# A diffusion trunk's GLA layers: level products at plain priority, larger first shares, gates dealt out between states

## The chip, the cores and the metric

The kernel runs on one core of a Trainium2 chip, as one launch. The metric is device time in microseconds, the median of several runs.

## The reference, cut to what matters

The model is a trunk of four layers over 512 latent and 256 context tokens of width 1024. Layer i uses mixer i % 3: layers 0 and 3 are gated linear attention (GLA), layer 1 is windowed attention, layer 2 a gated linear recurrence. Only the GLA layers are touched here. Each has four heads with keys of 128 and values of 256, and runs in both directions:

```python
la_f, la_b = [split_heads(jax.nn.log_sigmoid(((h @ w_g1[d]) @ w_g2[d] + b_g[d])) / GLA_TAU, GLA_HEADS) for d in range(2)]
...
def step(s, inp):
    q_n, k_n, v_n, b_n = inp
    rel = b_n[:, :, :, None, :] - b_n[:, :, None, :, :]
    decay = jnp.exp(jnp.where(lower, rel, -jnp.inf))
    scores = jnp.einsum('bhtd,bhsd,bhtsd->bhts', q_n, k_n, decay)
    o = scores @ v_n + (q_n * jnp.exp(b_n)) @ s
    b_last = b_n[:, :, -1:, :]
    s = jnp.exp(b_last)[:, :, 0, :, None] * s + jnp.swapaxes(k_n * jnp.exp(b_last - b_n), -1, -2) @ v_n
    return s, o
...
return (o.astype(z.dtype) * jax.nn.silu(z)) @ w_out
```

In layer 0 latent and context tokens both give an output; in layer 3 the context only gives the state that the latent tokens start from.

## The kernel before

All large products are made of three matmuls on a high and a low part of each operand, so each weight tile is split after its load: ScalarE copies the high half (line 266), VectorE or, for every third tile, GpSimd subtracts to get the low half (line 269). While `keep_pool` holds something, GpSimd gets none of these splits. Weight tiles `raw` and `wh`/`wl` have two buffers each.

A GLA layer (`gla`, from line 937 on) goes through its heads one after the other, and overlaps the outputs of one head with the preparation of the next:

- `gates(h)` (line 958): two small products per head and direction into two banks of PSUM (line 976), |x| and min(x, 0) (lines 980, 981), Exp, Ln, a subtraction (lines 982 to 984), a ladder of pairwise sums for the levels (line 987), and two more Exp (lines 988, 990). It gives the decay factors `tmp` and `ls`.
- `project(h)` (line 995): q and k, in three parts; the parts are q and k of the context (in layer 3 k alone), q of the latent tokens, and k of the latent tokens. `Y` holds k twice, once for each direction.
- `levels` (line 1038): the scores within a chunk of 128 are built from eight levels, of 1, 2, ... 128 tokens. `X` is q times a factor (line 1043). At each level up to 128, ScalarE copies k into `K` (line 1090, levels 2 to 16), TensorE makes many small products of 32 columns (`products`, line 1056, into the banks `sct`), and VectorE multiplies X and Y by the level's factors (line 1105). Then A is put together with masks on VectorE, GpSimd and ScalarE (lines 1116 to 1136).
- `outputs` (line 1138) of the head before: five pairs of transposes of Y (`turn`, line 1150) with copies to `kth` and `ktl` (lines 1152, 1153); five state products (`step`, line 1160) with their updates; then chunk products of A, values, X and states (line 1188), normalisation, and transposes into the output.
- `values(h)` and `zgates(h - 1)` (the silu gate z, line 395) are large products that are dealt out between the levels by `spread`: it hands each level a share of them and traces that share in front of the level's own instructions.
- `mods`: parts of the modulation products for later layers, whose weights come by DMA and whose matmuls have raised priority.

The order of work is not written out by hand here. Instructions are traced in the order of the Python code; a scheduler at build time fills each engine's queue, and takes of those instructions that it holds to be ready the one that was traced first. `tc.high_priority(n)` moves instructions up by n places in that order. On the chip each queue is then worked off strictly in that order, and an instruction that waits holds up all behind it on its engine. In the main loop before, `gates(h)` is called ahead of the projection and the states of the last head; `among` then runs two parts of the projection ahead of the outputs and one after the first state, and the level products are traced with priority 300.

Of the kernel before, what the change touches and what calls it, by code (L numbers as in the profile page):

```python
# [11 lines left out]
F32 = mybir.dt.float32  # L12
# [3 lines left out]
ALU = mybir.AluOpType  # L16
# [19 lines left out]
BURST = 300  # L36
# [41 lines left out]
def body(ctx: ExitStack, tc: tile.TileContext, I, out, layers=(0, 1, 2, 3)):  # L78
    nc = tc.nc
    V, S, G, PE = nc.vector, nc.scalar, nc.gpsimd, nc.tensor  # L80
# [59 lines left out]
    ps = pjt()  # L140
# [73 lines left out]
    keep_pool = []  # L214
# [77 lines left out]
    def load_g2(a, zero=True, load=True):  # L292

        r = gpt.rearrange("p j n -> p (j n)")[:, 0:1024].rearrange("p (d n) -> p d n", d=2)
        if a in g2_loaded:
            return r
        if zero:
            (V if a == 0 else G).memset(r, 0.0)
        if load:
            g2_loaded.append(a)  # L300
            for d in range(2):
                for g in range(3):
                    (nc.sync if d else nc.scalar).dma_start(
                        r[32 * g + 16 * d : 32 * g + 16 * d + 16, d, :], I["a_w_g2"][a, d]
                    )
        return r
# [281 lines left out]
    def run(steps):  # L588
        for _ in steps:
            pass  # L590
# [346 lines left out]
    def gla(i, a, ctx_out):  # L937
# [2 lines left out]
        TOT = 2 * T  # L940
        with phase(f"gla{i}") as mp:

            g2r = load_g2(a)
            w1 = weights("g1")
            t1 = mp.tile([P, T], F32R, name="t1")
            for stream in ("ctx", "lat"):
                t0, n = STREAM[stream]
# [6 lines left out]
            g2 = mp.tile([P, 2, 512], F32R, name="g2")  # L954
            S.copy(g2[:96], g2r[:96])
            G.tensor_tensor(g2[32:64], g2r[32:64], g2[32:64].bitcast(F32), op=ALU.subtract)

            def gates(h):


                tmp = mp.tile([P, 2, T], F32, name="tmp", tag="tmp")
                ls = mp.tile([P, TOT], F32, name="ls", tag="ls")

                def lev(n):
                    if n == 0:
                        return tmp
                    return ls[:, OFF[n] : OFF[n] + 2 * NLEV[n]].rearrange("p (d n) -> p d n", d=2)

                l1 = ls.rearrange("p (d n) -> p d n", d=2)
                for pl in range(2):  # L970
                    d = 1 - pl
                    b = sm[:, 48 + 8 * a + 4 * d + h : 49 + 8 * a + 4 * d + h]
                    ps = sct().rearrange("p c n -> p (c n)")
                    for stream in ("ctx", "lat"):
                        t0, n = STREAM[stream]
                        PE.matmul(
                            ps[:, t0 : t0 + n], g2[:96, d, h * P : (h + 1) * P], t1[:96, t0 : t0 + n],
                            start=True, stop=True,
                        )
                    S.activation(tmp[:, pl, :], ps[:, :T], AF.Abs, bias=b)  # L980
                    V.tensor_scalar(l1[:, pl, :], ps[:, :T], b, 0.0, op0=ALU.add, op1=ALU.min)
                S.activation(tmp, tmp, AF.Exp, scale=-1.0)
                S.activation(tmp, tmp, AF.Ln, bias=1.0)
                V.tensor_tensor(tmp, l1, tmp, op=ALU.subtract)
                for n in range(len(LEVELS) - 1):
                    s = lev(n).rearrange("p d (m two) -> p d m two", two=2)
                    V.tensor_tensor(lev(n + 1), s[:, :, :, 0], s[:, :, :, 1], op=ALU.add)
                S.activation(tmp, tmp, AF.Exp, scale=1.0 / 16.0)
                n = OFF[-1] + 2 * NLEV[-1]
                S.activation(ls[:, :n], ls[:, :n], AF.Exp, scale=1.0 / 16.0)  # L990
                tl = mp.tile([P, 2, NLEV[-1]], F32, name="tl", tag="tl", bufs=2)
                V.tensor_copy(tl, lev(len(LEVELS) - 1))
                return (tmp, ls), tl

            def project(h, q, Y):
                w = weights(f"qk{h}")
# [41 lines left out]
            def levels(ls, q, Y, X, A):  # L1038
# [42 lines left out]
                for n, L in enumerate(LEVELS):  # L1081
                    dims = ([2 * L, 16 // L], [T + L, 2], [1, L])
                    Ks = []
                    for chunks in groups if L < 128 else ():
                        k0, kn = chunks[0] * P, len(chunks) * P
                        if L == 1:
                            K = Y[:, 0, k0 : k0 + kn]
                        elif L <= 16:
                            K = mp.tile([P, 3 * P], F32, name="K", tag="K", bufs=2)
                            S.copy(K[:, :kn], view(Yf, k0, ([2 * L, kn // (2 * L)], [T + L, 2], [1, L])))  # L1090
                        else:
                            K = None
                        Ks.append((chunks, K))
                    with tc.high_priority(BURST):
                        for gi, (chunks, K) in reversed(list(enumerate(Ks))):
                            products(L, dims, tl[gi], chunks, K)
                    if L < 128:
                        N = NLEV[n]
                        lf = ls[:, OFF[n] : OFF[n] + 2 * N] if n else l1.rearrange("p d n -> p (d n)")

                        def up(Z, nt, off, step):
                            m = nt // (2 * L)
                            z = view(Z, 0, ([2 * L, m], [T + L, 2], [1, L]))
                            t = view(lf, off, ([2, m], [step, 2], [0, L]))
                            V.tensor_tensor(z, z, t, op=ALU.mult)

                        up(Xf, nq, 1, N - 1)
                        up(Yf, T, N + 1, -N - 1)
                    yield
# [28 lines left out]
            def outputs(h, X, Y, A, v, tl):  # L1138
# [5 lines left out]
                kt = {}  # L1144

                def turn(m):
                    ps = mxt()
                    for pl in range(2):
                        c = order[pl][m]
                        PE.transpose(ps[:, pl * P : (pl + 1) * P], Y[:, pl, c * P : (c + 1) * P], ident)  # L1150
                    kt[m] = [mp.tile([P, 256], F32R, name=n, tag=n, bufs=2) for n in ("kth", "ktl")]
                    S.copy(kt[m][0], ps[:, :256])
                    V.tensor_tensor(kt[m][1], ps[:, :256], kt[m][0].bitcast(F32), op=ALU.subtract)

                def step(m):
                    k = kt.pop(m)
# [85 lines left out]
            def mods(n):  # L1242
                for _ in range(n):
                    background(1)
                    yield
# [4 lines left out]
                    for stream in ("ctx", "lat") if ctx_out else ("lat",):  # L1250
                        yield from z_steps(mp, w, e, 2 * h + e, put, (stream,))

            def among(main, side, every, lead=0):

                for _ in range(lead):
                    next(side, None)
                for n, _ in enumerate(main):
                    if n in every:
                        next(side, None)

            def spread(main, side, steps, total):

                credit = 0
                for _ in range(steps):
                    credit += total / steps
                    while credit > 0:
                        credit -= next(side, 1e9)
                    next(main)
                run(main)

            put = {}
            prev = None
            keep_pool.append(1)
            for h in range(GH):
                ls, tl = gates(h)
                q = mp.tile([P, T], F32, name="q", tag="q")
                Y = mp.tile([P, 2, T], F32, name="Y", tag="Y", bufs=2)
                pr = project(h, q, Y)
                os = outputs(*prev) if prev else iter(())
                z = zgates(h - 1) if prev else iter(())  # L1280
                among(os, pr, [0, 3, 6], 2)
                run(pr)
                run(mods(3))
                X = mp.tile([P, 2, T], F32, name="X", tag="X")
                A = [mp.tile([P, 6, P], F32R, name=n, tag=n) for n in ("Ah", "Al")]
                lv = levels(ls, q, Y, X, A)

                if h < GH - 1:
                    OG.b = None
                    vl = OG.tail(F32R)  # L1290
                else:
                    vl = mp.tile([P, 2, T], F32R, name="vl", tag="tmp")
                v = (
                    mp.tile([P, 6, GDV], F32R, name="v", tag="v"),
                    vl.rearrange("p d t -> p (d t)").rearrange("p (c n) -> p c n", c=6),
                )

                side = chain(z, values(h, v))
                nz = len(STREAM) * T if ctx_out else len(STREAM) * TL
                nz = nz if prev else 0  # L1300
                spread(lv, side, len(LEVELS), 24 * (nz + 4 * GDV) / 2.4)
                run(side)
                run(mods(2))
                prev = (h, X, Y, A, v, tl)
# [459 lines left out]
```

## Time and profile before

| | |
|---|---|
| median of 3 runs | 1525.08 us (1524.38 to 1532.94) |
| the profiled execution | 1530.24 us |
| its span | 1528.5 us |
| TensorE busy | 1449.4 us (95%) |
| VectorE busy | 1013.6 us (66%) |
| ScalarE busy | 786.9 us (51%) |
| GpSimd busy | 190.5 us (12%) |
| mean granted TensorE clock | 0.983 |

The page gives for each engine its busy time and share of the span; a wait is named by the engine that sat idle and by the instruction that released it. All positions are microseconds from the span's start. In rows, PE is TensorE, DVE is VectorE, ACT is ScalarE, POOL is GpSimd and SP the queue that issues most DMAs; `L1160` is line 1160. PEclk is the granted clock, 1.00 for 2.4 GHz and 0.50 for 1.2 GHz. Layer 0's GLA runs from about 62 to 375 us, layer 3's from about 1225 to 1478 us.

### The profile page before, as it was taken

The numbers are of one execution on the slowest core, as the hardware profiler recorded it, in microseconds if no ns is written. First come the engines' busy times: TensorE is split into PE (matmuls) and PEld (weight loads), VectorE is DVE, ScalarE is ACT, GpSimd is POOL, SyncE is SP. The second block draws the span as 40 slices with busy tenths as digits, with TensorE's granted clock in tenths as the row PEclk, the third lists the DMA queues.
The fourth block names the chain that finished last, engine by engine and source line by source line (L and its number), as shares of the span: only waits on it lengthen the run. The fifth ranks groups of instructions, "written<-read, shape, count | busy, mean of one in ns | idle before, by whom it ended". The sixth has DMA issues, their size and how long they took to land.

```text
span 1528.5 us, 29077 instructions
## 1 busy us (share of the span) xinstructions
PE 1449.4 (95%) x11691; PEld 1213.7 (79%) x11691; DVE 1013.6 (66%) x1913; ACT 786.9 (51%) x1543; POOL 190.5 (12%) x301
## 2 busy tenths in 40 slices
PE   5998899999999899999999999899999889999998
PEld 3877788888877777878888787788878778879886
DVE  5585647576264389787883568988962666766754
ACT  4644353524252357655662477878842555355242
POOL 2211101012122200010000210000011311101111
PEclk8999999999999999999999999999999999999999
DMA  9450514112573632122216624212251352121132
GB/s 304 138 149 18 170 56 143 56 33 70 206 235 128 183 94 70 43 66 56 56 45 226 216 82 150 82 49 70 66 188 50 102 158 88 33 59 56 60 110 84
DMA packets 153046, 162.35 MB, mean 106 GB/s; under 512 B 12418, under 2 KB 141968, under 8 KB 152912
## 3 DMA queue, kind: packets, MB, share of 16 engines
q1 hardware_dynamic: 147456, 146.56, 31.0%
q10 hardware_dynamic: 5456, 13.94, 2.5%
q8 instruction: 92, 1.51, 0.4%
q14 instruction: 42, 0.34, 0.1%
HBM read 138.44 MB, written 11.53 MB: 98 GB/s over the span
## 4 chain that ended last, share of the span: by engine, by line
PE 51%; DVE 10%; ACT 7%; DMA 5%; issue 2%; SPq 1%; POOL 1%; ACTq 0%; DVEq 0%; POOLq 0%
PE mxt L796 15%; PE pjt L395 9%; PE pjt L385 6%; PE pjt L1028 4%; PE mxt L1525 3%; PE mxt L1509 2%; DMA raw<-in_w_mod_dram 2%; PE mxt L524 2%; PE sct L1630 2%; PE mxt L1468 1%; PE mxt L1188 1%; PE mxt L1451 1%; DVE wl L269 1%; ACT wh L266 1%; PE mxt L638 1%
## 5 line engine op out<-in xcount | busy, mean ns | idle before, releaser
L385 PE MATMUL pjt<-Rh,wh 128*128 128x256 f32 (+1 forms) x592 | 198.6, 337 | 7.1 <-DVE Rh L649 4.6
L385 PE MATMUL pjt<-Rl,wh 128*128 128x256 f32 (+1 forms) x592 | 198.1, 336 | 2.1 <-DVE Rl L650 1.8
L385 PE MATMUL pjt<-Rh,wl 128*128 128x256 f32 (+1 forms) x592 | 197.2, 334 | 0.7 <-DVE wl L269 0.7
L269 DVE TENSOR_TENSOR wl<-raw,wh 128x1024 fp32r<-128x1024 f32 x105 | 128.4, 1231 | 56.8 <-ACT wh L266 56.4
L266 ACT CAST wh<-raw 128x1024 fp32r<-128x1024 f32 x118 | 122.0, 1053 | 80.8 <-PE mxt L796 33.0
L395 PE MATMUL pjt<-Rl,wh 128*128 128x512 f32 (+1 forms) x448 | 162.0, 362 | 0.0
L395 PE MATMUL pjt<-Rh,wh 128*128 128x512 f32 (+1 forms) x448 | 161.6, 361 | 0.0
L395 PE MATMUL pjt<-Rh,wl 128*128 128x512 f32 (+1 forms) x448 | 161.3, 360 | 0.0
L796 PE MATMUL mxt<-wh,Rh 128*128 128x512 f32 x352 | 138.9, 395 | 0.0
L796 PE MATMUL mxt<-wh,Rl 128*128 128x512 f32 x352 | 137.6, 391 | 0.8 <-DVE Rl L769 0.8
L796 PE MATMUL mxt<-wl,Rh 128*128 128x512 f32 x352 | 137.2, 390 | 0.0
L385 PEld LDWEIGHTS pjt<-Rh,wh 128*128 128x128 f32 x592 | 112.6, 191 | 19.7 <-DVE Rh L649 5.7
L385 PEld LDWEIGHTS pjt<-Rl,wh 128*128 128x128 f32 x592 | 112.7, 191 | 15.9 <-DVE Rl L650 4.1
L385 PEld LDWEIGHTS pjt<-Rh,wl 128*128 128x128 f32 x592 | 112.7, 191 | 12.5 <-DVE wl L269 1.2
L1028 PE MATMUL pjt<-wh,Rh 128*128 128x256 f32 x384 | 110.8, 289 | 1.9 <-ACT wh L266 1.9
L1028 PE MATMUL pjt<-wl,Rh 128*128 128x256 f32 x384 | 110.3, 287 | 1.1 <-DVE wl L269 1.1
L1028 PE MATMUL pjt<-wh,Rl 128*128 128x256 f32 x384 | 110.2, 287 | 0.0
L1487 ACT ACTIVATE pe<-mxt,mxs 128x256 f32<-128x256 f32 (+2 forms) x128 | 70.7, 556 | 54.0 <-DVE mxs L1479 53.1
L395 PEld LDWEIGHTS pjt<-Rh,wl 128*128 128x128 f32 x448 | 86.0, 192 | 9.2 <-issue 1.9
L395 PEld LDWEIGHTS pjt<-Rh,wh 128*128 128x128 f32 x448 | 86.3, 193 | 8.7 <-issue 1.2
L395 PEld LDWEIGHTS pjt<-Rl,wh 128*128 128x128 f32 x448 | 86.2, 193 | 8.5 <-issue 1.3
L1477 DVE TENSOR_REDUCE mxs<-mxt 128x1 f32<-128x256 f32 (+2 forms) x128 | 65.4, 518 | 24.1 <-PE mxt L1468 10.5
(297 smaller groups left out, 3458.1 us busy)
## 6 DMA issues: line engine op xcount, KB each, us to landing
rawp<-in_w_mod_dram SPq DMA_DIRECT2D x48, 512.0 KB, 5.7
raw<-in_w_mod_dram SPq DMA_DIRECT2D x48, 512.0 KB, 3.7
raw<-in_a_w_in_dram SPq DMA_DIRECT2D x32, 512.0 KB, 3.5
raw<-in_b_w_in_dram SPq DMA_DIRECT2D x20, 512.0 KB, 5.1
raw<-in_c_w_in_dram SPq DMA_DIRECT2D x20, 512.0 KB, 3.7
xd<-x SPq DMA_DIRECT2D x18, 512.0 KB
raw<-in_a_w_out_dram SPq DMA_DIRECT2D x16, 512.0 KB, 3.4
x<-xd ACTq DMA_DIRECT2D x16, 512.0 KB, 8.2
```

The lines of the kernel that those rows point to most:

```text
L266: S.copy(h, x)
L269: e.tensor_tensor(l, x, h.bitcast(F32), op=ALU.subtract)
L385: PE.matmul(ps, w[u][:, k, c0 : c0 + P], R[v][:, k, t0 : t0 + n], start=(k == 0 and u + v == 0), stop=(k == KC - 1 and u == 1),)
L395: PE.matmul(ps, w[u][:, k, c0 : c0 + P], R[x][:, k, t0 : t0 + n], start=(k == 0 and u + x == 0), stop=(k == KC - 1 and u == 1),)
L524: PE.matmul(ps[32 * g : 32 * g + 32, 0:256], sT[:, k, :], r2[k // 4][:, k % 4, :], start=(n < 4), stop=(n >= 4), skip_group_check=True,)
L796: PE.matmul(ps, l[:, tt * P : (tt + 1) * P], r, start=(k == 0 and u + v == 0), stop=(k == kc - 1 and u == 1),)
L1028: PE.matmul(ps[:, n, :], R[u][:, k, tt * P : (tt + 1) * P], w[x][:, k, :], start=(k == 0 and u + x == 0), stop=(k == KC - 1 and u == 1),)
L1477: V.tensor_reduce(mxs[:, n : n + 1], u[e][:, :w], axis=AX.X, op=ALU.max)
L1487: S.activation(p[:, o : o + w], u[e][:, :w], AF.Exp, bias=nm, scale=0.125, accum_out=den[:, n : n + 1],)
L1509: PE.transpose(u[e][:, c * P : (c + 1) * P], ps[e][:, m * P : (m + 1) * P], ident)
L1525: PE.matmul(po[64 * e : 64 * e + 64, 0:P], v[:, keys[m], 64 * kv : 64 * kv + 64], pt[:, e, m * P : (m + 1) * P], start=(m == len(keys) - 1 ...
L1630: PE.matmul(ps[:, t0 : t0 + nn], wg[a][:, n, :], x[c][:, p0 : p0 + nn], start=(q == 0), stop=(q == 2),)
```

## The change

It alters the order only; the instructions stay what they were. Level products lose their raised priority. `spread` gives its first two shares 1.4 times the mean and the others less, with the same sum. `gates` becomes a generator with five steps, and leaves its result in `gated`; its steps are taken one after each state of the last head. The projection's first part is traced ahead of the first transpose (`turn(0)`), the second behind it, the third after the third round of the loop over the outputs. The copies `kth` and `ktl` get priority 300. `keep_pool` is set at the start of the layer and no longer just in front of the heads.

```diff
         with phase(f"gla{i}") as mp:
+            keep_pool.append(1)
             g2r = load_g2(a)
...
+            gated = {}
             def gates(h):
...
                     V.tensor_scalar(l1[:, pl, :], ps[:, :T], b, 0.0, op0=ALU.add, op1=ALU.min)
+                    yield
                 S.activation(tmp, tmp, AF.Exp, scale=-1.0)
+                yield
                 S.activation(tmp, tmp, AF.Ln, bias=1.0)
                 V.tensor_tensor(tmp, l1, tmp, op=ALU.subtract)
+                yield
...
-                return (tmp, ls), tl
+                gated[h] = (tmp, ls), tl
...
-                    with tc.high_priority(BURST):
-                        for gi, (chunks, K) in reversed(list(enumerate(Ks))):
-                            products(L, dims, tl[gi], chunks, K)
+                    for gi, (chunks, K) in reversed(list(enumerate(Ks))):
+                        products(L, dims, tl[gi], chunks, K)
...
-                    S.copy(kt[m][0], ps[:, :256])
-                    V.tensor_tensor(kt[m][1], ps[:, :256], kt[m][0].bitcast(F32), op=ALU.subtract)
+                    with tc.high_priority(300):
+                        S.copy(kt[m][0], ps[:, :256])
+                        V.tensor_tensor(kt[m][1], ps[:, :256], kt[m][0].bitcast(F32), op=ALU.subtract)
...
-            def among(main, side, every, lead=0):
-                for _ in range(lead):
-                    next(side, None)
-                for n, _ in enumerate(main):
-                    if n in every:
-                        next(side, None)
...
-                for _ in range(steps):
-                    credit += total / steps
+                for n in range(steps):
+                    credit += total / steps * (1.4 if n < 2 else (steps - 2.8) / (steps - 2))
...
-            keep_pool.append(1)
             for h in range(GH):
-                ls, tl = gates(h)
+                gt = gates(h)
...
-                among(os, pr, [0, 3, 6], 2)
+                next(pr)
+                next(os, None)
+                next(pr)
+                for n, _ in enumerate(os):
+                    next(gt, None)
+                    if n == 2:
+                        next(pr, None)
+                run(gt)
                 run(pr)
+                ls, tl = gated.pop(h)
```

## Rows read from the trace of the kernel before

**Rows 1.** GLA stretches: length, busy (count) of PE, PEld, DVE, ACT, POOL, clock, DMA
```profile
62.20:375.00 312.80, 297.47 (x3413) 257.99 (x3412) 203.72 (x326) 141.09 (x252) 37.85 (x68) 0.98 0.29 89
...
1225.00:1477.60 252.60, 242.79 (x2476) 209.21 (x2475) 173.47 (x273) 121.17 (x207) 28.13 (x60) 1.00 0.24 73
```
**Rows 2.** Waits of TensorE, layer 0, 62.2 to 375: us, times, longest
```profile
PE mxt L1160 <- DVE ktl L1153: 4.6, 1, 4.6
PE sct L1056 <- ACT K L1090: 3.6, 4, 1.1
PE pjt L1028 <- ACT wh L266: 1.9, 1, 1.9
PE mxt L524 <- DMA raw<-in_w_mod_dram: 1.8, 4, 0.6
PE pjt L1028 <- DVE wl L269: 1.1, 1, 1.1
```
**Rows 3.** Waits of TensorE, layer 3, 1225 to 1477.6
```profile
PE sct L1056 <- ACT K L1090: 2.7, 3, 0.9
PE sct L1056 <- ACT Y L1001: 2.5, 1, 2.5
PE mxt L524 <- DMA raw<-in_w_mod_dram: 2.4, 2, 1.3
PE sct L1056 <- DVE X L1105: 1.2, 1, 1.2
```
**Rows 4.** Timeline of ScalarE, layer 0 head 1: start, us, instruction, idle before
```profile
116.45 0.51 ACT L1135 CAST Ah<-A 128x384 fp32r<-128x384 f32 x1 [3.01 <-POOL A L1133]
...
118.86 1.28 ACT L983 ACT_TABLE_LOAD   x1
120.16 1.48 ACT L983 ACTIVATE tmp<-tmp 128x1536 f32<-128x1536 f32 x1
121.54 0.35 ACT L1152 CAST kth<-mxt 128x256 fp32r<-128x256 f32 x1
```
**Rows 5.** Timeline of VectorE at the same place
```profile
121.67 1.76 DVE L984 TENSOR_TENSOR tmp<-ls,tmp 128x1536 f32<-128x1536 f32 x1 [5.50 <-ACT tmp L983]
123.35 0.42 DVE L1153 TENSOR_TENSOR ktl<-mxt,kth 128x256 fp32r<-128x256 f32 x1
```
**Rows 6.** Busy time and clock in the two stretches at 1.2 GHz, layer 0
```profile
122.60:129.43 6.83, 5.61 (x27) 5.33 (x28) 3.94 (x10) 4.99 (x6) 0.00 (x0) 0.50 0.00 0
...
170.38:177.21 6.83, 5.86 (x67) 5.47 (x68) 5.20 (x7) 1.80 (x3) 0.00 (x0) 0.50 0.54 154
```
**Rows 7.** Timeline of the SP queue, layer 0 head 1
```profile
165.18 9.06 SPq L229 DMA_DIRECT2D raw<-in_a_w_in_dram  x6
```
**Rows 8.** Timeline of TensorE, layer 0 head 0: one wait for K
```profile
87.11 0.40 PE L1056 MATMUL sct<-X,K 128*32 128x32 f32 x24 [0.96 <-ACT K L1090]
```
**Rows 9.** Line 385 alone: the projection of layer 0 head 2 on TensorE
```profile
195.84:207.07 11.23, 11.23 (x72) 10.08 (x71) 1.00 0.35 112
207.20:212.76 5.56, 5.56 (x25) 4.41 (x24) 1.00 0.00 0
```
**Rows 10.** Line 395 alone: z within the states and chunks of head 2
```profile
212.90:231.70 18.80, 7.81 (x38) 5.59 (x38) 1.00 0.00 1
```
**Rows 11.** Timeline of ScalarE, layer 0 head 2: first and last gate work, K
```profile
195.81 1.70 ACT L980 ACTIVATE tmp<-sct,sm 128x768 f32<-128x768 f32 x2
...
208.33 1.48 ACT L990 ACTIVATE ls<-ls 128x1524 f32<-128x1524 f32 x1
...
236.07 1.01 ACT L1090 COPY K<-Y 128x384 f32<-128x384 f32 x2 [0.83 <-DVE modT L543]
```
**Rows 12.** Timeline of VectorE, layer 0 head 2: X and level 1
```profile
229.70 1.76 DVE L1043 TENSOR_TENSOR X<-tmp,q 128x1536 f32<-128x1536 f32 x1 [1.72 <-PE mxt L1188]
...
232.92 1.64 DVE L1105 TENSOR_TENSOR X<-X,tmp 128x768 f32<-128x768 f32 x1
234.40 1.65 DVE L1105 TENSOR_TENSOR Y<-Y,tmp 128x768 f32<-128x768 f32 x1
```

## The prediction

> **What bounds the kernel now.** I first read the page: TensorE is busy for 95% of the span and heads the chain that ended last, while no other engine passes 66%. So a change of order can gain only TensorE's own waits, and what a lowered TensorE clock costs after a long one. Second, the table by stretch: in the two GLA layers TensorE is idle 312.80 - 297.47 = 15.3 us and 252.60 - 242.79 = 9.8 us [rows 1], 25 us together. The rest of the kernel is not touched. Third, TensorE's waits in these stretches [rows 2, 3], with the timelines of the engines that release them.
>
> The reader is to see four kinds. (a) One wait of 4.6 us in head 1 of layer 0: the first state product waits for the low half of a transposed key. ScalarE did not copy the high half until 121.54, because in its queue stood a copy of A that came late from GpSimd, the gates' table load (1.28 us) and their Ln (1.48 us) [rows 4]; on VectorE the gates' subtraction of 1.76 us stood ahead as well [rows 5]. After it the granted clock is 0.50 (1.2 GHz) for 6.83 us, in which TensorE works 5.61 us [rows 6]; at 2.4 GHz that is half, so the clock costs 2.8 us. (b) 1.9 + 1.1 us in the same head, where the values wait for their weights, again with a stretch at 1.2 GHz holding 5.86 us of work, a cost of 2.9 us [rows 2, 6]. Their load was issued only at 165.18, behind the modulation loads in the two raw buffers [rows 7]. (c) Level products that wait for the copy K: 3.6 us in layer 0, 2.7 in layer 3, all at the second or a later level [rows 2, 3]. Of the 3.6, 1.0 belongs to head 0 [rows 8]. (d) 2.5 us in layer 3 for the copy Y: with raised priority four products of level 1 stand early in TensorE's queue and block what follows until Y is there [rows 3].
>
> **The change part by part.** No instruction is added or taken away; every part changes only in what order the engines' queues are filled. The sum therefore consists of waits.
>
> *Key copies at priority 300, gates dealt out.* Ahead of head 1's states ScalarE no longer has the gates' Exp, Ln and table load: gates are now traced from the first state product on. The transposes of turn 0 come after the first part of the projection, and their copies go ahead of what waits on ScalarE and VectorE. What is late next there would be the state products themselves; the last projection product of 5.56 us [rows 9] is now traced among them and fills their gaps, and z (38 products, 7.81 us, in head 2 [rows 10]) behind it. I take (a) in full: 4.6 + 2.8 = 7.4 us.
>
> The price is that the gates start later in the six heads that follow another. In head 2 they take from 195.81 to 208.33 + 1.48 = 209.81 on ScalarE, 14.0 us [rows 11], all beneath the projection's 11.23 us and the next 5.56 us [rows 9]. Now they start after 11.23 us and one state product, and X, which needs them, starts today 229.70 - 195.84 = 33.9 us after the projection began [rows 9, 12]. 11.2 + 14.0 = 25.2 us leaves 8.7 us for that product and for delays. X may itself come earlier by the z that leaves the states, at most 7.8 us [rows 10]; even then the gates stay hidden, by the states, the last projection product and z. If that cover were gone, each late us would cost a us per head.
>
> But the key copies, which used to find a quiet ScalarE, now meet the gates among them. Priority puts a copy ahead of a waiting gate step, not of a running one. Bounds per head: nothing, where k's product or z covers it; or a table load and an Ln in front of one copy, 1.28 + 1.48 = 2.8 us [rows 4], in six heads 16.6 us. A gain below nothing is excluded: in heads 2 and 3 TensorE has no wait in that stage to give back [rows 2, 3]. I take 0.5 us a head, 3.0 us, near the lower end, because five copies a head meet two table loads and filler stands behind all five.
>
> Row and rule differ on this price. The trace has the Ln starting at 120.16, straight behind a load of 1.28 us that began at 118.86 [rows 4]. The Trainium skill (ScalarE: Activation LUTs, "What ACT_TABLE_LOAD costs" and "Table sets: the hidden batching unit") tells one to batch activations by table set, since every switch costs about 1.28 us and a drain of about 1.38 us on top; dealing Exp, Ln and Exp out between other work goes against it. By that rule the upper bound would be six times 2.66 + 1.48, 24.8 us, as an estimate from that page, and the forecast would lose its sign at that end; the row here shows no drain, so 16.6 us is used.
>
> *Level products without raised priority, first two shares 1.4 times.* Today level 2's products come as soon as the planned order thinks K is ready; VectorE's two multiplications for level 1 take 1.64 + 1.65 us from 232.92 on [rows 12], and K follows. A share of z and values is 24 x (1536 + 1024) / 2.4 ns = 25.6 us over eight levels, 3.2 us by the spread's own count; the first two become 4.5 us and stand in front of the products, longer than the 3.3 us and one K copy, half of the 1.01 us for two [rows 11]. Later shares shrink to 2.8 us, against multiplications of half the elements. In layer 3 the shares are 2.6 and 3.6 us, and X is two thirds as wide. So (c) vanishes in heads 1 to 3 of both layers: 3.6 - 1.0 + 2.7 = 5.3 us. Lower bound: nothing, if K is still late. In head 0 no z stands by and a share is 1.3 us; there the order goes by readiness as before and I take nothing of its waits, 1.0 us for K and 1.2 for X [rows 3, 8]. The wait (d) goes too, since the four early products lose their place: 2.5 us. Levels last longer by this, eight shares of 3.2 us and their products; what hides the finishing of A behind them is the last third of the values and the next projection's first 11.23 us [rows 9].
>
> *The weights of (b).* The chain behind it, three modulation parts and then the load, starts when the outputs end and is not changed. But k's product replaces z as filler of the states, so up to 5.6 us more z is left when the levels begin, against a wait of 2.9 us. Bounds: nothing, and 2.9 + 2.9 = 5.8 us; I take half, 2.9 us, since a z that stays longer is just about what is missing.
>
> *keep_pool set earlier.* At most the low half of one weight tile in layer 3 moves from GpSimd to VectorE, in a place where TensorE still has the projection to do; nothing. The waits for modulation weights (1.8 and 2.4 us [rows 2, 3]) keep their raised priority and stay.
>
> **Sum:** 7.4 + 5.3 + 2.5 + 2.9 - 3.0 = 15.1 us. From the profiled execution, 1530.24 us around a span of 1528.5, this gives 1515.1. That execution lies 5.2 us above the median of the runs, 1525.08; so the forecast is 1525.1 - 15.1 = **1510 us**.
>
> **Rivals.**
> *Better:* (b) goes in full (2.9 more), the dealt-out gates cost nothing (3.0) and head 0's two waits (2.2) go as well: 23.2 us, 1502. For it: the filler is ample. Against: nothing in the change reaches head 0.
> *Key copies late behind gates:* the price is the upper 16.6 us instead of 3.0, which leaves 1.5 us of gain: 1523.5. For it: exactly this pair stood in each other's way in head 1 [rows 4]. Against: priority 300, and that a filler is traced behind each step.
> *The waits move on:* the products do go later, but z runs out earlier in the levels, so that (b) stays whole, and half of (c) comes back as waits for X or for the values' weights: 15.1 - 2.9 - 2.6 = 9.6 us, 1515.5. For it: the levels now last longer. Against: the count of z left, above.
> *Slower:* the values' weights come late in every head. They take the slot of the projection's weights, which is now free only after the third projection part, inside the states, and their conversion stands beside the gates. If they land after z has run out, each of six heads pays what head 1 paid in (b), 5.9 us: 35 us, less the 18 us gained, 1542. It decides where the delay exceeds the z left at that point. Against it: the wait on wh and wl occurs in one head of eight today [rows 2, 3].
>
> **How the numbers follow.** Forecast 0.50, better 0.14, key copies late 0.18, waits move on 0.09, slower 0.09. The range takes better and the rivals up to 1523.5, with about 3 us for (b) left whole: 1500 to 1527, the forecast's own being 1504 to 1516. A difference of 1%, 15.3 us, is about what a measurement of this kernel can tell from no change; the line lies at 1509.8, so half of the forecast's chance lies on either side. Faster: 0.25 + 0.14 = 0.39. Within 1%: 0.25 + 0.18 + 0.09 = 0.52. Slower: 0.09.
>
> **What the profile afterwards would show.** Right: no wait of TensorE on ktl in head 1 and no clock of 0.50 near 123 us; the K waits gone in heads 1 to 3; Y's wait of 2.5 us gone; the gates' ScalarE rows between the key copies; GLA stretches of about 301 us (7.4 + 2.9 + 2.6 less three heads' price) and 249 us. The price would be seen as new waits of state products on kth or ktl, each of about 1 us or less. Wrong: state products that wait several us in each head, X waiting for the gates' Exp, or values waiting on wh in more heads than one.

## The result, and the profile after

The changed kernel takes 1516.7 us (median of 10 runs) against 1526.2 us (10 runs) of the kernel before, a ratio of 0.994 [0.992, 0.996]: 9.5 us less, where 15.1 were forecast. The profiled execution took 1513.6 us around a span of 1511.8. Line numbers behind 940 are some 3 to 6 higher than before (the key copies are L1158 and L1159, the level products L1062, level multiplications L1110, K L1096, state products L1166, the transposes L1155); in the experiments they differ by a few lines again.

The two GLA layers, cut by head: first the kernel before, then the changed one. Columns: stretch, length, TensorE's busy time (instructions), granted clock, DMA share, GB/s. The first five rows are layer 0 (heads 0 to 3 and what follows the last), then heads 0 and 1 of layer 3. A head ends with the last product of its values. The four gate products of the next head, some 0.7 us, lie behind that border now and lay before it (those of head 1 of layer 0 lay behind it before, too). Lengths in the text are taken between the unrounded borders.

```profile
62.10:95.50 33.40, 31.17 (x472) 1.00 0.52 149
95.50:195.80 100.30, 89.96 (x1076) 0.93 0.34 109
195.80:272.10 76.30, 75.28 (x869) 1.00 0.28 88
272.10:344.00 71.90, 70.60 (x812) 1.00 0.15 47
344.00:374.70 30.70, 30.26 (x191) 1.00 0.17 52
1205.30:1272.00 66.70, 59.27 (x648) 0.95 0.46 144
1272.00:1335.40 63.40, 59.41 (x602) 1.00 0.18 53
...
```

```profile
62.20:96.50 34.30, 30.86 (x423) 0.95 0.51 153
96.50:188.30 91.80, 84.59 (x1120) 1.00 0.38 119
188.30:264.70 76.40, 75.28 (x870) 1.00 0.28 85
264.70:338.30 73.60, 71.80 (x817) 1.00 0.15 46
338.30:370.00 31.70, 30.42 (x190) 1.00 0.16 50
1194.70:1258.60 63.90, 58.98 (x644) 0.95 0.48 150
1258.60:1319.60 61.00, 60.10 (x603) 1.00 0.18 55
...
```

Layer 0 went from 312.5 to 307.9 us, layer 3 (its last three stretches, 142.1 us before, are 141.2 now) from 272.2 to 266.1: 10.7 us together. Another 5.3 us by which the two executions differ lie in layer 1, which the change doesn't touch (last section). Head 1 of layer 0 alone is 8.5 us shorter (0.7 of it by the border), 5.4 of it busy time, which is mostly clock (0.93 to 1.00), and 3.1 idle time. Heads 2, 3 and the end of layer 0 got longer by 2.8 us.

How much of this is clock can be estimated as the prediction does it in (a): half of TensorE's busy time at 1.2 GHz. That is 5.7 us in layer 0 and 3.1 in layer 3 before, 1.7 and 2.9 now. Without it layer 0 went only from 306.8 to 306.2 us, and layer 3 from 269.1 to 263.2: what the new order itself gave lies mostly in layer 3.

TensorE's waits in head 1 of layer 0, where [rows 2] had 4.6 us for ktl and 1.9 + 1.1 for wh and wl (waited for: us, times, longest):

```profile
PE mxt L1166 <- ACT st L1177: 1.6, 1, 1.6
PE mxt L524 <- DMA raw<-in_w_mod_dram: 1.4, 2, 0.9
PE mxt L1155 <- DVE ktl L1159: 1.2, 1, 1.2
PE mxt L1166 <- DVE ktl L1159: 0.9, 1, 0.9
PE mxt L1155 <- DVE Y L1110: 0.8, 1, 0.8
...
```

The waits of (b) are gone, with their stretch at 1.2 GHz. In the place of the 4.6 us of (a) stand four waits of 1.6, 1.2, 0.9 and 0.8 us, 4.5 in all, spread over the states between 109 and 131 us. In this execution no clock of 0.50 [rows 6] followed them. ScalarE's timeline shows where the 1.6 us come from (start, us, instruction, idle before):

```profile
115.69 0.36 ACT L1158 CAST kth<-mxt 128x256 fp32r<-128x256 f32 x1
119.05 0.51 ACT L1140 CAST Ah<-A 128x384 fp32r<-128x384 f32 x1 [3.00 <-POOL A L1138]
119.47 0.64 ACT L1177 COPY st<-mxt 128x256 f32<-128x256 f32 x2
120.00 0.92 ACT L983 ACTIVATE tmp<-sct,sm 128x768 f32<-128x768 f32 x1
120.80 0.38 ACT L1158 CAST kth<-mxt 128x256 fp32r<-128x256 f32 x1
```

The first two of the five key copies now run early, at 110.92 and 115.69. But the copy Ah behind them still waits 3.00 us for GpSimd, as it did before [rows 4], and the state copy, for which TensorE waits 1.6 us, and the third key copy stand behind it in the queue. The 1.2 us have another cause: on VectorE the second low half stands behind a weight split.

```profile
115.75 1.72 DVE L269 TENSOR_TENSOR wl<-raw,wh 128x1024 fp32r<-128x1024 f32 x1
117.39 0.41 DVE L1159 TENSOR_TENSOR ktl<-mxt,kth 128x256 fp32r<-128x256 f32 x1
```

In layer 3 the waits for K and Y of [rows 3] are gone from heads 1 to 3; the 0.8 us left belong to head 0:

```profile
...
PE mxt L1166 <- DVE st L1179: 0.9, 1, 0.9
PE sct L1062 <- ACT K L1096: 0.8, 1, 0.8
```

In head 0 of layer 0, where I had counted on nothing, one wait for K of 3.4 us stands where 1.0 stood [rows 8], and 3.41 us at 1.2 GHz follow it. VectorE's timeline there:

```profile
82.72 1.23 DVE L269 TENSOR_TENSOR wl<-raw,wh 128x1024 fp32r<-128x1024 f32 x1 [2.33 <-ACT wh L266]
...
85.00 1.64 DVE L1110 TENSOR_TENSOR X<-X,tmp 128x768 f32<-128x768 f32 x1
86.47 1.22 DVE L269 TENSOR_TENSOR wl<-raw,wh 128x1024 fp32r<-128x1024 f32 x1
87.60 0.41 DVE L576 TENSOR_TENSOR ml<-gb,mh 128x256 fp32r<-128x256 f32 x1
87.92 0.69 DVE L1042 TENSOR_TENSOR OGb<-pjt,v 128x512 fp32r<-128x512 f32 x1
88.52 1.65 DVE L1110 TENSOR_TENSOR Y<-Y,tmp 128x768 f32<-128x768 f32 x1
```

The gates of head 0 now follow its first two projection parts; X's multiplication falls behind a weight split that stands 2.33 us for ScalarE, and Y's behind three more operations. K is copied when Y is done.

### The profile page after: what moved, and what is told of

Its sections match the earlier page's. It is cut to its first block, busy times and chain, and to the rows that moved or that the text cites. A ratio compares the mean times of both kernels' runs of the same rounds, so it can differ in the third digit from the quotient of the medians.

```text
span 1511.8 us, 29077 instructions
## 1 busy us (share of the span) xinstructions
PE 1442.0 (95%) x11691; PEld 1206.4 (80%) x11691; DVE 1010.5 (67%) x1914; ACT 784.2 (52%) x1541; POOL 189.4 (13%) x300
## 4 chain that ended last, share of the span: by engine, by line
PE 54%; DVE 10%; ACT 5%; DMA 4%; issue 2%; SPq 1%; POOL 1%; ACTq 0%; DVEq 0%; POOLq 0%
PE mxt L796 14%; PE pjt L395 9%; PE pjt L385 9%; PE pjt L1034 4%; PE mxt L1532 3%; PE mxt L1516 2%; PE sct L1637 2%; PE mxt L524 1%; PE mxt L1475 1%; PE mxt L1194 1%; DVE wl L269 1%; PE mxt L1458 1%; DMA bb<-in_b_mod_dram 1%; DMA raw<-in_w_mod_dram 1%; PE sct L1062 1%
## 5 line engine op out<-in xcount | busy, mean ns | idle before, releaser
L395 PE MATMUL pjt<-Rh,wl 128*128 128x512 f32 (+1 forms) x448 | 160.3, 358 | 0.0
L395 PE MATMUL pjt<-Rl,wh 128*128 128x512 f32 (+1 forms) x448 | 159.8, 357 | 0.0
L395 PE MATMUL pjt<-Rh,wh 128*128 128x512 f32 (+1 forms) x448 | 159.5, 356 | 0.0
L395 PEld LDWEIGHTS pjt<-Rh,wl 128*128 128x128 f32 x448 | 84.6, 189 | 9.8 <-issue 1.9
L395 PEld LDWEIGHTS pjt<-Rh,wh 128*128 128x128 f32 x448 | 84.7, 189 | 9.2 <-issue 1.2
L395 PEld LDWEIGHTS pjt<-Rl,wh 128*128 128x128 f32 x448 | 84.7, 189 | 9.2 <-issue 1.3
L804 DVE TENSOR_TENSOR y<-mxt,gpt 128x512 f32<-128x512 f32 x44 | 30.3, 689 | 73.9 <-ACT y L803 73.8
```

What stands on the lines that cost most here:

```text
L395: PE.matmul(ps, w[u][:, k, c0 : c0 + P], R[x][:, k, t0 : t0 + n], start=(k == 0 and u + x == 0), stop=(k == KC - 1 and u == 1),)
L804: V.tensor_tensor(y[tt][:, c], ps, gpt[:, 1 if tt >= 4 else 0, c], op=ALU.mult)
```

## The experiments

The GLA columns are lengths in the profiled execution, cut as above. The last column is both layers less what the clock costs there, by the estimate above. Two pairs of kernels have the same order of work in these layers: before and shares_only, but for one product of z, and the changed kernel and pool_late, but for one weight split at the start of layer 3. Their lengths differ by 1.5 and 4.2 us, as more or fewer stretches at 1.2 GHz fell into them; without the clock both layers together differ by 0.1 and 0.5 us, a single layer by up to 1.6. Whole runs of one kernel scatter by several us. Ratios are to the kernel before on the same chip. Ratio and lengths part by 3 to 4 us in gates_kt, proj_kt, gates_oldproj and gates0_first, so what follows rests on the named waits and on the last column, not on a length or a ratio alone.

| kernel | ratio [95%] | layer 0 | layer 3 | both without clock |
|---|---|---|---|---|
| before | 1 | 312.5 | 272.2 | 575.9 |
| changed | 0.994 [0.992, 0.996] | 307.9 | 266.1 | 569.4 |
| shares_only | 1.001 [0.999, 1.003] | 313.0 | 273.2 | 576.0 |
| prio_shares | 1.005 [1.003, 1.007] | 315.6 | 277.0 | 583.3 |
| kt_only | 0.998 [0.996, 0.999] | 308.6 | 272.2 | 575.4 |
| gates_kt | 0.993 [0.991, 0.996] | 311.7 | 266.3 | 572.2 |
| gates_only | 0.996 [0.994, 0.998] | 311.6 | 266.4 | 572.1 |
| proj_kt | 1.001 [1.000, 1.002] | 310.8 | 277.2 | 581.6 |
| gates_oldproj | 0.997 [0.995, 0.999] | 311.5 | 273.2 | 576.7 |
| gates0_first | 0.998 [0.996, 0.999] | 312.7 | 271.4 | 577.5 |
| gk_prio | 0.994 [0.991, 0.997] | 310.5 | 266.1 | 573.2 |
| pool_late | 0.995 [0.993, 0.997] | 310.4 | 267.8 | 569.9 |
| diag_dve | 0.991 [0.989, 0.993] | 305.1 | 266.1 | 566.4 |
| up1 | 0.991 [0.987, 0.994] | 305.0 | 266.2 | 566.5 |

**The level products: shares_only and prio_shares.** The kernel before with the last edit, then with the last two:

```diff
-                    credit += total / steps
+                    credit += total / steps * (1.4 if n < 2 else (steps - 2.8) / (steps - 2))
```
```diff
-                    with tc.high_priority(BURST):
-                        for gi, (chunks, K) in reversed(list(enumerate(Ks))):
+                    for gi, (chunks, K) in reversed(list(enumerate(Ks))):
```

> The kernel before with only the first two shares raised to 1.4 times; products keep their raised priority. If the share alone covers the wait for K (the forecast's reading of the 5.3 us), the seven K waits of heads 1 to 3 fall and the time falls by 3 to 5 us, to about 1521. If raised priority makes the share idle (products jump the share as soon as they count as ready), the K waits stay at 3.6 and 2.7 us and the time stays within 1 us of before, about 1526; its profile then also shows how far layer 1, which is not touched, differs between two executions of the same order.

> The kernel before with the level products at plain priority and the first shares at 1.4 times; gates and key copies as before. Theory 1 (head 1's gain belongs to gates and key copies): the wait on ktl of 4.6 us and the clock of 0.50 near 123 us stay, the K waits of heads 1 to 3 and the wait for Y go: 4 to 6 us faster, about 1521. Theory 2 (the order of the products is what sets head 1 too): 8 us or more faster, 1518 or below.

The shares alone change nothing: the order of the queues stays as it was but for one product of z, so under raised priority the size of the filler's share has no effect. Both together make the kernel slower, by 7.9 us in the GLA layers (7.4 without the clock) and 0.5% in the runs, where both of my theories had it faster. Layer 3, heads 1 to 3:

```profile
PE mxt L1149 <- ACT st L1170: 3.1, 1, 3.1
PE sct L1056 <- ACT K L1090: 2.7, 3, 0.9
```

All three K waits stand as in [rows 3], and the wait for Y has only become one of a transpose for a state copy, longer than the one it replaced. So these edits by themselves bring neither (c) nor (d).

**Gates and key copies: gates_kt, kt_only, gates_only.** gates_kt is the changed kernel with products' priority and shares as before; kt_only is the kernel before with the key copies at priority 300; gates_only is gates_kt without that:

```diff
-                    with tc.high_priority(300):
-                        S.copy(kt[m][0], ps[:, :256])
+                    S.copy(kt[m][0], ps[:, :256])
```

> The kernel before with gates dealt out, the projection's new order, key copies at priority 300 and keep_pool early; level products and shares as before. Theory 1: head 1 of layer 0 gives its 8 us, head 0 pays 1 us, the K waits of 3.6 and 2.7 us stay: 5 to 7 us faster, about 1520. Theory 2 (products set it): within 2 us of before.

> Only the key copies at priority 300, all else as before. If the 4.6 us wait for ktl came of the copy's place in ScalarE's queue alone: head 1 of layer 0 5 to 7 us shorter, nothing else, 1519 to 1521 us. If the queue is full ahead of it in any order (a copy of A that waits for GpSimd, the gates' table load and Ln): under 1.5 us, 1525 to 1526 us.

> Gates dealt out and the projection dealt anew, key copies at ordinary priority; products' priority and shares as before. If the priority is needed to keep the gates' table loads and Ln from in front of the key copies: new waits of state products on kth or ktl of 1 to 2.8 us in most of the six heads, 1521 to 1530 us. If the copies come in time anyway: 1516 to 1519 us, as with the priority.

Dealing out the gates and the projection gives almost the whole of layer 3's gain, without either edit that I had credited: Y's wait is gone, and of the three K waits one of 0.5 us is left, in head 1. In layer 0 it removes no K wait (below). The key copies' priority alone shortens the layers by 3.9 us (head 1 of layer 0 goes from 100.4 to 95.4), but only by 0.5 without the clock: head 1 then has one stretch at 1.2 GHz instead of two. With the gates dealt out it adds nothing: gates_only and gates_kt both come to 578.0 us. Neither clears the way for the states of head 1: TensorE still waits there for ktl for 3.9 us in gates_kt, 1.9 + 1.6 in gates_only and 2.1 + 0.4 in kt_only.

**Which half: proj_kt and gates_oldproj.** The edit moves two things, the gates and the projection's parts. proj_kt keeps the new projection and puts a head's gates in front of it in one go; gates_oldproj deals out the gates but leaves the projection's parts in their old places. The products' priority and the shares are as before in both; proj_kt has the key copies at priority 300, gates_oldproj has not. The first edit is shown against gates_kt, the second against gates_only:

```diff
+                run(gt)
                 next(pr)
                 next(os, None)
```
```diff
                 next(pr)
-                next(os, None)
                 next(pr)
                 for n, _ in enumerate(os):
+                    if n in (0, 3, 6):
+                        next(pr, None)
                     next(gt, None)
-                    if n == 2:
-                        next(pr, None)
```

> The new dealing of the projection and the key copies at priority 300, but each head's gates in one go ahead of its projection; products' priority and shares as before. Theory 1 (dealing out the gates is what gains): the state products of head 1 in layer 0 wait for ktl again, layer 3's waits for K and Y return, 1524 to 1528 us. Theory 2 (the gain is the projection's: k's product among the states and more z left for the levels; where the gates stand hardly matters): no waits for K in heads 2 and 3 of layer 3, 1516 to 1520 us.

> Gates dealt out between the last head's states, but the three projection parts in their old places (two ahead of the outputs, the third behind the first transposes); key copies at ordinary priority, products' priority and shares as before. With the kernel that has the gates dealt out and the projection dealt anew, and the one that has only the projection dealt anew, it says whether the gates' new place alone makes the gain. If it does: layer 3's waits for K and Y gone, that layer 266 to 267 us, the program 1516 to 1520 us. If the third projection part among the states is needed as filler: the states wait for kth or ktl in most heads, and layer 3 stays at 270 us or more, 1522 to 1530 us.

Neither half does it. Layer 3 is 277.2 and 273.2 us with one of them, 272.2 with none, 266.4 with both (gates_only). Waits in heads 1 to 3 of layer 3, proj_kt first, then gates_oldproj:

```profile
PE mxt L1156 <- DVE ktl L1160: 3.2, 1, 3.2
PE sct L1062 <- ACT K L1096: 3.0, 3, 1.0
PE sct L1062 <- ACT Y L1007: 1.3, 2, 0.7
...
```
```profile
PE sct L1062 <- ACT K L1096: 2.2, 3, 0.8
...
```

What the pair changes can be counted: the products of z (L395 alone) in head 2 of layer 3, from the head's start to level 1, and from level 1 to level 2, for before, proj_kt, gates_oldproj and gates_only (columns as in [rows 9]):

```profile
1335.40:1366.80 31.40, 8.73 (x29) 5.02 (x29) 1.00 0.23 68
1366.80:1371.10 4.30, 2.43 (x9) 1.43 (x8) 1.00 0.17 34
...
```
```profile
1332.40:1360.80 28.40, 4.18 (x13) 2.23 (x13) 1.00 0.25 75
1360.80:1365.10 4.30, 2.36 (x8) 1.43 (x8) 1.00 0.12 34
...
```
```profile
1324.70:1363.10 38.40, 13.47 (x48) 8.51 (x48) 1.00 0.18 55
1363.10:1367.40 4.30, 0.00 (x0) 0.00 (x0) 1.00 0.12 34
...
```
```profile
1324.80:1354.60 29.80, 6.32 (x22) 3.99 (x22) 1.00 0.24 71
1354.60:1360.10 5.50, 3.78 (x15) 2.48 (x14) 1.00 0.11 27
...
```

Only with both do 15 products of z stand between levels 1 and 2, and the stretch lasts 5.5 us instead of 4.3, which covers the multiplications and the copy of K. With the projection in its old place the states of the dealt-out kernel end later (the last starts 30.8 us into the head, 24.3 before), and all 48 z run before level 1 and leave none. With the gates in front, z is left (13 used), but the plan still puts level 2 behind 8. Why the plan does so I can only argue: with the gates in VectorE's queue late, it also reckons K later. The count is shown, that reason is not.

**gk_prio, pool_late.** The changed kernel with equal shares, and with the keep_pool line in its old place:

```diff
-                    credit += total / steps * (1.4 if n < 2 else (steps - 2.8) / (steps - 2))
+                    credit += total / steps
```
```diff
-            keep_pool.append(1)
             g2r = load_g2(a)
...
+            keep_pool.append(1)
             for h in range(GH):
```

> The changed kernel with equal shares (only the 1.4 is taken back): gates dealt out, key copies at priority 300, level products without raised priority. It tells which of the last two edits makes the 3.7 us by which head 1 of layer 0 is shorter in the changed kernel than with the gates and key copies alone. If the plain priority: 1516 to 1518 us, the GLA layers together 574 us. If the larger first shares: 1520 to 1522 us, 578 us or more. Without the shares the K waits of layer 3 should come back if it was the shares that removed them there: 3 waits of 0.9 us; I expect none.

> The changed kernel with the line on the low halves (keep_pool) back where it stood, behind the layer's first weight loads. The prediction gave it nothing. If so: 1515 to 1518 us and the GLA layers within 1 us of the changed kernel's 574 us. Rival: the queues are planned anew behind the moved half and the GLA layers differ by 2 us or more either way.

In length the plain priority takes 1.4 us from the 578.0 of gates_kt and the shares 2.6 more, and head 1 of layer 0 goes from 96.1 to 94.8 to 91.8 us; without the clock the priority gives nothing (573.2 against 572.2) and the shares 3.8. The runs can't tell the three apart (intervals above). The waits say what the two edits do together. TensorE's waits for K in layer 0 in gates_kt, gk_prio and the changed kernel, the longest of each in head 0:

```profile
PE sct L1062 <- ACT K L1096: 8.0, 4, 4.0
```
```profile
PE sct L1062 <- ACT K L1096: 6.1, 5, 3.2
```
```profile
PE sct L1062 <- ACT K L1096: 4.7, 2, 3.4
```

So heads 1 to 3 keep 4.0, 2.9 and 1.3 us, where the kernel before had 2.7. The one wait left in layer 3's head 1, 0.5 us in gates_kt and 0.8 in gk_prio, goes with the shares, too.

keep_pool's line, worth nothing by my forecast, is worth nothing by the order: pool_late has the changed kernel's order but for the one split, and 569.9 against 569.4 us without the clock. Of the 4.2 us between the two executions 3.7 are clock (8.3 against 4.6): my rival had the size and not the reason. In head 1 of layer 0 the same waits of 1.2 and 1.6 us stand in both, but in pool_late's execution TensorE then ran at 1.2 GHz for 6.83 us:

```profile
121.59:128.42 6.83, 5.84 (x18) 0.50 0.19 65
```

Differences of 2 to 4 us in length between such kernels can be clock alone, and no single edit should be paid for them.

**Head 0's gates first: gates0_first.**

```diff
+                if not prev:
+                    run(gt)
                 next(pr)
```

> The changed kernel, but in each layer's head 0 all gates are traced ahead of the projection, as before. Theory: the new wait of 3.4 us for K in head 0 of layer 0, with its 3.4 us at 1.2 GHz, comes from gates that start 1.1 us later, so that level 1's multiplications fall behind a weight split on VectorE; it goes, and head 0 takes 2 to 3 us less than in the changed kernel; in layer 3 head 0 gates run 8 us earlier and nothing is gained. About 1514. Rival: the split stands in front by readiness of its load whatever the gates do; the wait stays and the time is within 1 us of the changed kernel's 1516.7.

Head 0's K wait in layer 0 does shrink, from 3.4 to 0.8 us. But head 1 got 5.4 us longer (a wait for ktl of 3.7 us is back) and head 0 of layer 3 4.7 us. Neither of my two cases came: the kernel is slower than the changed one, by 10 us in the GLA layers of the profiled executions (8.1 without the clock) and by 0.4% in the runs.

**A's diagonal sums on VectorE: diag_dve.** The changed kernel, with the additions that the copy Ah waits for moved off GpSimd:

```diff
-                        G.tensor_tensor(o, o, dg[r, :nch, :], op=ALU.add)
+                        V.tensor_tensor(o, o, dg[r, :nch, :], op=ALU.add)
```

> The changed kernel, with the small diagonal sums of A on VectorE in place of GpSimd (all four of a group, 32 partitions each). Theory: ScalarE's 3.0 us wait at the copy Ah in head 1 of layer 0 is what makes the state copy and the low key half late there (1.6 + 1.2 us); it goes, 2 to 3 us less than the changed kernel, about 1514 us. Rival: VectorE gets later by as much, 1516 to 1518 us.

Head 1 of layer 0, its row of the table and its longest wait for the states' inputs; then ScalarE's state copy and the copy Ah:

```profile
96.90:185.20 88.30, 84.49 (x1121) 1.00 0.38 119
```
```profile
PE mxt L1166 <- DVE ktl L1159: 1.6, 2, 1.1
...
```
```profile
115.79 0.65 ACT L1177 COPY st<-mxt 128x256 f32<-128x256 f32 x2
...
118.36 0.51 ACT L1140 CAST Ah<-A 128x384 fp32r<-128x384 f32 x1 [0.86 <-DVE A L1138]
```

Ah now waits 0.86 us and stands behind the state copy, TensorE's wait for the state copy is gone, and the head takes 88.3 us, 3.5 less. Of these, 1.9 us lie in the waits of the states, 4.5 in the changed kernel and 2.6 here, and most of the rest in waits for modulation work, which the experiment doesn't tie to Ah. Both layers without the clock come to 3.0 us less. With 1511.8 us (4 runs), 0.991 of the kernel before, this is the best version of the study together with up1; its interval [0.989, 0.993] just overlaps the changed kernel's. The same additions by line, in the changed kernel and here (busy us, mean ns):

```profile
L1138 POOL TENSOR_TENSOR A<-A,dg 32x96 f32<-32x96 f32 (+1 forms) x64 | 25.7, 401 | 182.9 <-DVE dg L1131 149.3 <-PE mxt L542 30.8
```
```profile
L1138 DVE TENSOR_TENSOR A<-A,dg 32x96 f32<-32x96 f32 (+1 forms) x64 | 14.8, 232 | 0.9
```

They take 232 ns instead of 401. The Trainium skill (GPSIMD Engine Reference, "4.1 Engine selection") puts elementwise work with two inputs on VectorE, GpSimd being about twice as slow; the rows agree, with 1.7.

**Level 1 earlier: up1.** diag_dve with the first two multiplications of each head at priority 100:

```diff
+                        with tc.high_priority(100 if n < 1 else 0):
                             up(Xf, nq, 1, N - 1)
                             up(Yf, T, N + 1, -N - 1)
```

> The version with the diagonal sums on VectorE, and with level 1's two multiplications of X and Y at priority 100. Theory: in head 0 of layer 0 they stand behind weight splits, a modulation sum and a split of the values in VectorE's queue, so K comes 3.2 us late and the clock falls to 0.50; ahead of them the wait is under 1 us and the half clock goes: 4 to 6 us less than that version, 1506 to 1508 us. Rival: the work that they pass comes late in its turn (the values' weights, the modulation), or the order of the other heads turns worse, as when head 0's gates went first: 1511 to 1516 us.

Y now follows X directly, past the second weight split, a modulation operation and the split of the values. But X still stands behind the first weight split, idle for 2.03 us until ScalarE's copy is there, and TensorE runs out of work sooner: K is 3.1 us late in head 0, with 1.2 GHz behind it again. Head 0 gains 1.4 us and head 2 1.4, head 1 pays 2.6 (modulation weights, waits of 1.2 and 1.8 us): level with diag_dve, also without the clock. The rival was right.

## Why the prediction came out as it did

The direction and the range held. The main idea, gates away from in front of the key copies, held only in part: without the clock 3.7 of the 6.5 us come with gates, projection and key copies (gates_kt) and 2.8 with the last two edits on top, and the gates and the projection gain by layer 3's waits for K and Y, hardly by the key copies of layer 0. The forecast of 1510 us lay 6.7 below the time. By its steps:

- **(a), forecast 7.4 us.** The 4.6 us of waiting did not come: four waits of 4.5 us stand in their place, and without the last two edits (gates_kt) one of 3.9. The clock's 2.8 us came in the profiled execution and not in that of pool_late, which has the same order and ran 6.83 us at 1.2 GHz there; that part was luck. The failed step is "What is late next there would be the state products themselves; the last projection product [...] fills their gaps". What was late next stood in the first line of [rows 4]: Ah, 3.01 us for GpSimd, which the change doesn't touch. I struck the Ln and the table load behind it and left Ah out of the sum. diag_dve takes away the longest of the four waits, 1.6 us, and its head is 3.5 us shorter.
- **(b), forecast half of 5.8 us.** All of it came: no wait for wh or wl in head 1, no 1.2 GHz there. Here the rival's fuller amount was right. The reason given, more z left for the levels, isn't shown: kt_only, which leaves the projection in its old place, has only 0.2 us of this wait in head 1.
- **(c), forecast 5.3 us.** Layer 3's 2.7 us came in full. In layer 0, heads 1 to 3 had 0.6 and 2.1 us and keep 1.3. So 4.1 us, near the forecast, but only in part for its reason. The step "Level products without raised priority, first two shares 1.4 times" fell with prio_shares, which keeps layer 3's waits and loses 7.9 us. In heads 2 and 3 of layer 3 the waits go through the gates and the projection together. In layer 0 and in head 1 of layer 3 the step holds, but only on top of that pair: with the pair alone (gates_only) layer 0's waits rise to 3.6 us.
- **(d), forecast 2.5 us.** It came, again through the gates and not through the priority: gates_only and gates_oldproj have no wait for Y there.
- **Price of the dealt-out gates, forecast 3.0 us.** Heads 2, 3 and the end of layer 0 are 2.8 us longer, 0.7 of that being the border of the heads, though 0.8 us of K waits went. Only one wait of 0.9 us there is for ktl; the rest is modulation weights (0.9), chunks (0.9) and 0.7 us of busy time; that this is more switching between small and large products is not shown. The size held, the place did not. In layer 3 the price is one state wait of 0.9 us. No table load was added (8 at either place, before and after), and in diag_dve the Ln starts at 122.77, straight behind a load of 1.28 us from 121.48: the drain of the Trainium skill's rule (ScalarE: Activation LUTs, "What ACT_TABLE_LOAD costs") is not seen here either.
- **Head 0, forecast nothing.** Wrong in layer 0: 2.4 us more for K, and 3.41 us at 1.2 GHz, because its gates moved as well. "Against: nothing in the change reaches head 0" overlooked that the gates are now traced behind the first projection parts in every head; in gates0_first, which takes that back, the wait is 0.8 us. In layer 3's head 0 it went the other way: the wait for X of 1.2 us [rows 3] is gone and the modulation waits are half, and the head is 2.8 us shorter, 0.7 of it by the border, which I had not counted.
- **keep_pool, forecast nothing.** Right: the order stays, and without the clock 0.5 us lie between the kernels with and without it.

Layer 3 thus gave 6.1 us where 3.7 were forecast, and layer 0 4.6 where 11.4 were; without the clock it is 5.9 and 0.6. The GLA stretches of [rows 1], forecast as "about 301 us" and 249, became 307.9 us and, from 1214 to 1461.3, 247.3.

## What to carry over

When a wait is taken off an in-order queue, go through every instruction that stood in front of the late one, with its own releaser, and ask which is last once the named one is gone; a copy that waits for a slow engine blocks whatever priority the next one has. What filler remains where it is wanted is a matter of counting products between two landmarks, and two moves that look separate can each be worth nothing alone. The same order can differ by 4 us between two profiled executions through the clock alone, so single edits of a bundle should be credited by an experiment that is read by its waits, with the clock's cost taken off, and not by a length or by the story that fits them.

## What the runs showed of the chip

A wait of 4.6 us in head 1 was followed by 6.83 us at 1.2 GHz [rows 6], and the wait of 3.4 us in head 0 by 3.41 us at that clock, while four waits of 0.8 to 1.6 us in the changed head 1 left the granted clock at 1.00. That is not a matter of their size alone: pool_late has waits of 1.2, 1.2 and 1.6 us in the same order there, and its clock fell to 0.50 for 6.83 us with 5.84 us of work, as it did beside the waits of 1.9 and 1.1 us of (b). After waits of this size the clock fell in one execution and not in another, and 2.9 us (half of 5.84) hang on it.

Layer 1, whose instructions no kernel here changes, took from 420.1 to 429.5 us between executions, as stretches at 1.2 GHz fell in it or not (17.1 us of them in up1, none in gates_oldproj). In gates_oldproj and in up1 (columns as in the first table):

```profile
373.80:793.90 420.10, 406.11 (x3033) 1.00 0.37 110
```
```profile
367.80:797.30 429.50, 413.08 (x3034) 0.98 0.36 107
```

Busy time differs by 7.0 us for the same products. So two single executions can differ by several us with nothing changed: the spans of before and after differ by 16.7 us, their medians by 9.5.
